# Dilated-attention projections regrouped from twelve 384-wide blocks to nine 512-wide ones, with both query tiles of a head pair scored together

## The chip, the cores and the metric

The kernel runs on one core of a Trainium2 chip. The metric is the device time in microseconds (us) of one launch; the compute engines of the core are TensorE (PE, its weight loads are listed as PEld), VectorE (DVE), ScalarE (ACT) and GpSimd (POOL), and SyncE (SP) issues the DMA transfers. A lower time is better.

## What is computed

Four transformer-like layers work on one activation `x` of 256 rows by 1024 columns in float32: one attention layer, one retention layer (each with a gated feed-forward part), and then two "hybrid" layers. Only the hybrid layers are touched here. One hybrid layer, cut to what matters:

```
h = rmsnorm(x, norm_g)
proj = h @ w_in                                  # 1024 x 11168
a_b, a_c, a_x, a_z, c_q, c_kv, k_pe, b_z, dq, dk, dv, c_z, gate_pre = split(proj)
# a: gated short convolution, b: latent attention (MLA)
# c: dilated attention: 3 groups (dilation 1, 4, 16) x 8 heads x 64
dq = rmsnorm(dq per head); dk = rmsnorm(dk per head)
for g in 3 groups:                               # causal, ALiBi bias, window/dilation
    o_g, lse_g = dilated_group_attention(dq[g], dk[g], dv[g], slopes[g], dilation_g)
o_c = sum_g softmax_g(lse_g) * o_g               # = one softmax over the keys of all groups
y_c = o_c * silu(c_z)
merged = g_a*(y_a @ w_out_a) + g_b*(y_b @ w_out_b) + g_c*(y_c @ w_out_c)
x = x + merged @ w_o
```

The columns `dq`, `dk` and `dv` are 1536 each: 3 groups by 8 heads by 64. The change concerns how these 4608 columns are projected and how the dilated heads are scored.

## The kernel before

The 256 rows are two row tiles `t` of 128. Every large product is computed in three passes of split float32 (a high and a low part of both operands; `mm3` issues high by high, high by low, low by high). The activation `h` is the operand that is loaded (128x128) and the weights stream past it, 512 or 384 or 416 columns at a time, into one PSUM bank of 512 float32 columns; there are eight banks (`bank`, tag `p`). A weight block is loaded by SP in raw chunks (`raw`, line 325, two buffers), and ACT makes the high part (`whi`, line 345) and DVE the low part (`wlo`, line 346) in pieces of up to 1024 elements a partition; eight pieces are held at once (`WB`).

`gemm_col` walks over the blocks of columns: for each block, row tile 0 and then row tile 1, eight k steps of three matmuls each. When a row tile of a block is complete, its epilogue (`epi`) is spawned as a job, a Python generator, which issues some work and then yields a planned delay (`D_DQ`, `D_SOFTD`, ...). The PE's order is that in which the program issues its instructions: a planner adds the modelled time of every matmul to a clock, and after each `mm3` the jobs whose time is due issue their next piece, so that small matmuls and transposes (`trs`, line 281, one 128x128 transpose for each 128 columns) are interleaved between the large ones. PE executes exactly this order and waits where an operand is not ready; the other engines' order is made by a scheduler from the same program order.

In a hybrid layer `first_half` does the convolution and the MLA branch. Then `dilated` runs over four head pairs `pr`. For each pair there are three weight blocks of 384 columns (3 groups by 128): q, k and v. The q and k epilogues square the bank (ACT, `dsq`), sum by head (DVE, `dss`), take the inverse root (POOL, line 452), scale into `rows` (DVE), and `D_DQ` = 7.82 planned us later transpose `rows` (3 transposes) into `dq` or `dk`, with even and odd sequence positions apart. The v epilogue copies the bank (`dvn`) and two DMAs separate even and odd rows into `dv`. `dq`, `dk`, `dv` have two buffers each.

When all epilogues of a pair are done, `dil_pair` spawns `dil_heads` for query tile 0 (even positions), and 2 * `SP_DIL` = 9 planned us later for tile 1 (odd positions). One `dil_heads` scores both heads of the pair: 8 matmuls of 64 rows by 128 columns, which the profile shows as 16 (float32 runs as two), into two banks; the heads sit on partitions 0 to 63 and 64 to 127, so two run side by side. Then for each head there is bias and maximum (DVE, line 1388), exponential with sum (ACT, line 1390), reciprocal, scaling (ACT, line 1392) into `dsm`, and `D_SOFTD` = 5.7 planned us after the scores four transposes for head 0 and, `D_SOFTD2` = 2.2 later, four for head 1, copied to `daT`. The values product of a tile (again 16 matmuls in the profile, 64 columns of output each, `p<-daT,dv`) is issued when that tile's job is done. `ocT` receives the pair's result; it is needed in the third branch, after the blocks `c_z` of the projection.

After the dilated blocks come 512-wide blocks of the same projection: `b_z` (epilogue due after `D_Z` = 12.44), two gate blocks, and so on.

Of the kernel before, what the change touches and what calls it, by code (L numbers as in the profile page):

```python
# [21 lines left out]
NEG = -1e30  # L22
BIG = 1e30
WB = 8
AT0, DSM, DAT, GT = 8, 4, 4, 2
# [7 lines left out]
D_EV0, D_ROT0, D_SOFT, D_SB = 5.11, 5.49, 11.39, 9.42  # L33
D_ADA0, D_ADAF, D_ADA1, D_FFN, D_FFN1 = 12.84, 50.82, 20.9, 11.5, 11.36
D_ROT, D_GG, D_B0, D_Q, D_K, D_EV, D_SOFTM = 9.55, 13.08, 3.75, 17.27, 6.36, 5.2, 8.78
D_DQ, D_SOFTD, D_SOFTD2, D_Z, D_MERGE = 7.82, 5.7, 2.2, 12.44, 1.98
SP_SB, SP_MB, SP_MLA, SP_DIL = 2.55, 2.65, 13.59, 4.5

def _r(a, b):
    return list(range(a, b))
# [14 lines left out]
B_CONV, B_GA, B_DIL, B_ZB, B_GB, B_ZC, B_GC = 1, 5, 7, 19, 20, 22, 23  # L57
# [177 lines left out]
DIL_COLS = [[(0, 1), (0, 0), (1, 0), (2, 0)], [(0, 1), (1, 1), (2, 1), (0, 0)]]  # L235
# [9 lines left out]
class Kern:  # L245
# [1068 lines left out]

    def dilated(self, q, gqk, ocT):
        V, A, wk = self.V, self.A, self.wk
        pj = []
        for pr in range(4):
            dq, dk = (q.tile([128, 3, 256], F32, tag=n, bufs=2, name=self.nm(n)) for n in ("dq", "dk"))
            dv = q.tile([128, 2, 384], F32, tag="dv", bufs=2, name=self.nm("dv"))  # L1320
            b0 = B_DIL + 3 * pr
            eo = lambda x, t: x.rearrange("p g (r t i) -> p g t r i", r=2, t=2)[:, :, t]

            def epi(b, t, _, ps, b0=b0, dq=dq, dk=dk, dv=dv):
                if b - b0 == 2:
# [4 lines left out]
                    return  # L1330
                sq = wk.tile([128, 512], F32, tag="rtmp", name=self.nm("dsq"))
                ss = wk.tile([128, 8], F32, tag="dss", bufs=4, name=self.nm("dss"))
                rows = wk.tile([128, 512], F32, tag="rows", bufs=4, name=self.nm("rows"))
                A.activation(sq[:, :384], ps, AF.Square, scale=0.125)  # L1334
                V.tensor_reduce(ss[:, :6], sq[:, :384].rearrange("p (h d) -> p h d", d=64), AX.X, ALU.add)  # L1335
                self.rstd(ss[:, :6], 6, 1e-6)
                V.tensor_tensor(rows[:, :384].rearrange("p (h d) -> p h d", d=64), ps.rearrange("p (h d) -> p h d", d=64),  # L1337
                                ss[:, :6, None].to_broadcast([128, 6, 64]), ALU.mult)
                yield D_DQ
                src = self.trs(rows, 3).rearrange("p g (i r) -> p g r i", r=2)  # L1340
                if b == b0:
                    A.copy(eo(dq, t), src)
                else:
                    V.tensor_tensor(eo(dk, t), src, gqk[:, :, None, None].to_broadcast([128, 3, 2, 64]), ALU.mult)

            jb = self.gemm_col(self.h, self.key, self.chs[b0:b0 + 3], epi, b0)
            pj.append(self.spawn(self.dil_pair(pr, dq, dk, dv, ocT, jb), 0.5))
        return pj

    def dil_pair(self, pr, dq, dk, dv, ocT, deps):  # L1350


        tabs = []
# [19 lines left out]
        self.A.copy(ocT[:, pr].rearrange("p (n r) -> p r n", r=2), pv[:, :256].rearrange("p (r n) -> p r n", r=2))  # L1373

    def dil_heads(self, t, dq, dk, tabs, aTs):


        V, A = self.V, self.A
        ps = [self.bank() for _ in range(2)]
        for i, (g, k) in enumerate(DIL_COLS[t]):  # L1380
            for j, o in enumerate((0, 64)):
                self.mm(ps[j][:, i * 128:i * 128 + 128], dq[o:o + 64, g, t * 128:t * 128 + 128],
                        dk[o:o + 64, g, k * 128:k * 128 + 128], us=0.12)
        sms = []
        for j in range(2):
            st = self.wk.tile([128, 6], F32, tag="st", bufs=8, name=self.nm("dst"))
            sm = self.ph.tile([128, 512], F32, tag="dsm", bufs=DSM, name=self.nm("dsm"))
            V.tensor_tensor_reduce(sm, ps[j], tabs[j][:, t * 128:t * 128 + 512], 1.0, NEG, ALU.add, ALU.max, st[:, 0:1])  # L1388
            V.tensor_scalar_mul(st[:, 2:3], st[:, 0:1], -0.125)  # L1389
            A.activation(sm, sm, AF.Exp, bias=st[:, 2:3], scale=0.125, accum_out=st[:, 3:4])  # L1390
            V.reciprocal(st[:, 3:4], st[:, 3:4])
            A.activation(sm, sm, AF.Copy, scale=st[:, 3:4])  # L1392
            sms.append(sm)
        yield D_SOFTD
        for j in range(2):
            aT = self.ph.tile([128, 4, 128], F32, tag="daT", bufs=DAT, name=self.nm("daT"))
            A.copy(aT, self.trs(sms[j], 4))
            aTs[t, 64 * j] = aT
            yield D_SOFTD2 if j == 0 else 1.5


def build(tc, a, stop=99):
# [67 lines left out]
```

## Time and profile before

| | before |
|---|---|
| runs, us | 1496.15, 1497.75, 1500.12 |
| median, us | 1497.75 |
| profiled execution: time, us | 1494.65 |
| profiled execution: span of the instructions, us | 1492.9 |
| busy share of PE, DVE, ACT, POOL | 98%, 69%, 53%, 6% |
| PE instructions | 7508 |
| mean granted TensorE clock | 0.993 |

The span is the time from the first to the last instruction in the profiled execution; that execution's own time has a little added around it. A matmul's row in the timeline has its start and its length, and successive matmuls overlap, so the time that one takes from the stream is the distance from its start to the next start, not its length. In the names, `p<-whi,hh` means that the bank `p` is written from the weights `whi` and the activation `hh`.

### The profile page before, as it was taken

To read this page: it belongs to the slowest core of one execution; us is meant where nothing else is said; L and a number is where in the kernel's file an instruction comes from. 1 tells how busy PE (TensorE), PEld (TensorE's weight loads), DVE (VectorE), ACT (ScalarE), POOL (GpSimd) and SP (SyncE) were. 2 spreads that over 40 slices of the span, in tenths; PEclk is the share of its full clock that TensorE was granted. 3 is DMA by queue.
4 is the path that set the end of the run, shared out by engine and by line. 5 is a ranking of instruction groups with operands and counts; after the bars stand their busy time and mean duration, and the time that the engine had idled before them with its cause. 6 is when DMAs were issued, how large, how long until landed. Compare 5 with 4: busy or idle time off the path is not lost.

```text
span 1492.9 us, 19658 instructions
## 1 busy us (share of the span) xinstructions
PE 1458.3 (98%) x7508; PEld 1213.2 (81%) x7508; DVE 1022.9 (69%) x1605; ACT 793.8 (53%) x1297; POOL 96.3 (6%) x84
## 2 busy tenths in 40 slices
PE   7999999999999999999999999999999999999998
PEld 4776788887877888888887889988888889998887
DVE  4688887846988849755378655566676865656664
ACT  4657555533444535554266745566445674566551
POOL 0000000000000000000012011110001201111000
PEclk9999999999999999999999999999999999999999
DMA  9757587755776638645445455554635535555552
GB/s 379 273 177 275 193 324 285 285 199 184 279 276 231 258 137 279 256 174 197 155 144 180 146 170 178 181 202 154 220 135 200 190 121 194 171 179 198 184 174 80
DMA packets 52961, 306.62 MB, mean 205 GB/s; under 512 B 7546, under 2 KB 10490, under 8 KB 24580
## 3 DMA queue, kind: packets, MB, share of 16 engines
q1 hardware_dynamic: 52148, 305.14, 57.2%
q8 instruction: 59, 0.97, 0.3%
q10 hardware_dynamic: 720, 0.24, 0.1%
q14 instruction: 34, 0.28, 0.1%
HBM read 301.16 MB, written 1.05 MB: 202 GB/s over the span
## 4 chain that ended last, share of the span: by engine, by line
PE 75%; DVE 11%; ACT 5%; DMA 4%; POOL 3%; issue 2%; POOLq 0%; SPq 0%; DVEq 0%; ACTq 0%
PE p L277 71%; DVE wlo L346 5%; PE p L281 4%; DMA raw<-in_w_in_dram 3%; POOL dss L452 2%; ACT dsm L1390 1%; ACT whi L345 1%; DVE dsm L1388 1%; ACT dsm L1392 1%; DVE dss L1335 1%; POOL qss L452 1%; DVE junk L493 0%; DVE rows L1337 0%; ACT dsq L1334 0%; DVE res L520 0%
## 5 line engine op out<-in xcount | busy, mean ns | idle before, releaser
L346 DVE TENSOR_TENSOR wlo<-raw,whi 128x1024 fp32r<-128x1024 f32 (+2 forms) x474 | 539.6, 1161 | 163.5 <-ACT whi L345 158.1
L345 ACT CAST whi<-raw 128x1024 fp32r<-128x1024 f32 (+2 forms) x474 | 464.4, 1002 | 276.3 <-PE p L277 191.4
L277 PE MATMUL p<-whi,hh 128*128 128x512 f32 (+1 forms) x1504 | 590.9, 393 | 5.0 <-ACT mqT L1223 2.0
L277 PE MATMUL p<-whi,hl 128*128 128x512 f32 (+1 forms) x1504 | 568.3, 378 | 3.2 <-DVE hl L457 2.7
L277 PE MATMUL p<-wlo,hh 128*128 128x512 f32 (+1 forms) x1504 | 566.7, 377 | 0.0
L277 PEld LDWEIGHTS p<-whi,hh 128*128 128x128 f32 x1504 | 284.1, 189 | 55.3 <-issue 8.7
L277 PEld LDWEIGHTS p<-whi,hl 128*128 128x128 f32 x1504 | 283.8, 189 | 50.0 <-DVE hl L457 3.9
L277 PEld LDWEIGHTS p<-wlo,hh 128*128 128x128 f32 x1504 | 284.6, 189 | 40.9 <-issue 1.7
L541 DVE SCALAR_TENSOR_TENSOR acc<-raw,csc,acc 128x1024 f32<-128x1024 f32 x80 | 102.3, 1278 | 4.6 <-DMA raw<-in_ada_w_dram 4.3
L277 PE MATMUL p<-whi,ah 128*128 128x512 f32 x176 | 70.0, 398 | 0.0
L277 PE MATMUL p<-whi,al 128*128 128x512 f32 x176 | 69.5, 395 | 0.0
L277 PE MATMUL p<-wlo,ah 128*128 128x512 f32 x176 | 69.5, 395 | 0.0
L452 POOL TENSOR_TENSOR dss<-dss,mh 128x6 f32<-128x6 f32 x32 | 46.2, 1443 | 331.1 <-DVE dss L451 331.1
L916 ACT ACTIVATE fth<-p 128x256 f32<-128x256 f32 x44 | 16.9, 383 | 69.3 <-PE p L277 69.3
L1337 DVE TENSOR_TENSOR rows<-p,dss 128x384 f32<-128x384 f32 x32 | 17.8, 557 | 46.3 <-POOL dss L452 46.3
L1390 ACT ACTIVATE dsm<-dsm,dst 128x512 f32<-128x512 f32 x32 | 22.9, 716 | 40.8 <-DVE dst L1389 40.8
L485 POOL TENSOR_TENSOR ss<-ss,mh 128x1 f32<-128x1 f32 x14 | 13.5, 962 | 479.3 <-DVE ss L484 479.3
L277 PE MATMUL p<-whi,s 128*128 128x512 f32 x128 | 41.3, 397 | 0.0
L277 PEld LDWEIGHTS p<-whi,al 128*128 128x128 f32 x176 | 33.0, 187 | 8.1
L277 PEld LDWEIGHTS p<-wlo,ah 128*128 128x128 f32 x176 | 33.0, 188 | 7.8
L277 PEld LDWEIGHTS p<-whi,ah 128*128 128x128 f32 x176 | 33.0, 188 | 7.8
L277 PE MATMUL p<-whi,yh 128*128 128x512 f32 x96 | 38.4, 400 | 0.0
(251 smaller groups left out, 1522.3 us busy)
## 6 DMA issues: line engine op xcount, KB each, us to landing
raw<-in_w_in_dram SPq DMA_DIRECT2D x48, 1024.0 KB, 4.9
raw<-in_w_gu_dram SPq DMA_DIRECT2D x44, 1024.0 KB, 5.1
raw<-in_ada_w_dram SPq DMA_DIRECT2D x40, 1024.0 KB, 6.3
raw<-in_w_in_dram SPq DMA_DIRECT2D x48, 768.0 KB, 4.4
raw<-in_w_ret_dram SPq DMA_DIRECT2D x24, 1024.0 KB, 5.0
raw<-in_w_dn_dram SPq DMA_DIRECT2D x22, 1024.0 KB, 4.9
raw<-in_w_qkv_dram SPq DMA_DIRECT2D x11, 1024.0 KB, 5.5
as<-in_ada_s_dram SPq DMA_DIRECT2D x16, 512.0 KB, 8.0
```

The costliest lines, as they stand in the source:

```text
L277: self.T.matmul(out, lhsT=lhsT, rhs=rhs, start=first, stop=last, skip_group_check=skip)
L281: self.T.transpose(out, in_, self.ident)
L345: for ins in (self.A.copy(hi[:, :m * n], src), self.V.tensor_tensor(lo[:, :m * n], src, hi[:, :m * n].bitcast(F32), ALU.subtract)):
L346: self.V.tensor_tensor(lo[:, :m * n], src, hi[:, :m * n].bitcast(F32), ALU.subtract)):
L452: self.G.tensor_tensor(ss, ss, self.mh[:, :n], ALU.pow)
L541: self.V.scalar_tensor_tensor(acc, r[:, j * D:j * D + D], self.sc[:, k:k + 1], acc, ALU.mult, ALU.add)
L916: A.activation(th, ps[:, 0:256], AF.Silu)
L1335: V.tensor_reduce(ss[:, :6], sq[:, :384].rearrange("p (h d) -> p h d", d=64), AX.X, ALU.add)
L1337: V.tensor_tensor(rows[:, :384].rearrange("p (h d) -> p h d", d=64), ps.rearrange("p (h d) -> p h d", d=64), ss[:, :6, None].to_broadcast( ...
L1388: V.tensor_tensor_reduce(sm, ps[j], tabs[j][:, t * 128:t * 128 + 512], 1.0, NEG, ALU.add, ALU.max, st[:, 0:1])
L1390: A.activation(sm, sm, AF.Exp, bias=st[:, 2:3], scale=0.125, accum_out=st[:, 3:4])
L1392: A.activation(sm, sm, AF.Copy, scale=st[:, 3:4])
```

## The change

The nine (p, s, g) units of a head pair (q, k, v by three groups, 128 columns each) are put one after the other for all four pairs, 36 units in all, and cut into nine blocks of four units, 512 columns, in place of twelve blocks of 384. One epilogue serves a block with any mix of q, k and v units of one or two pairs: the q and k units of a block (4, 2, 3, 3, 2, 4, 1, 4 and 1 of them) are squared, normalised and transposed together, and then copied run by run into the buffers of their pair; v units are copied and sent by DMA run by run. A pair starts when all epilogues of the blocks that hold one of its units are done, that is after blocks 2, 4, 6 and 8.

`dil_heads` is gone. A pair issues the scores of both query tiles in one stretch (four banks, 32 matmuls as the profile counts them), the softmax of its four heads one behind the other, then the four groups of four transposes, the first `D_SOFTD` = 6.8 planned us after the scores and the others 2.4 apart, and then the values of both tiles in one stretch (32 matmuls). No arithmetic is changed.

```diff
-D_DQ, D_SOFTD, D_SOFTD2, D_Z, D_MERGE = 7.82, 5.7, 2.2, 12.44, 1.98
-SP_SB, SP_MB, SP_MLA, SP_DIL = 2.55, 2.65, 13.59, 4.5
+D_DQ, D_SOFTD, D_SOFTD2, D_Z, D_MERGE = 7.82, 6.8, 2.4, 12.44, 1.98
+SP_SB, SP_MB, SP_MLA = 2.55, 2.65, 13.59
...
-for _p in range(4):
-    for _b in (2976, 4512, 6048):
-        IN_BLOCKS.append([_b + g * 512 + _p * 128 + j for g in range(3) for j in range(128)])
+DIL_UNITS = [(p, s, g) for p in range(4) for s in range(3) for g in range(3)]
+for _i in range(0, 36, 4):
+    IN_BLOCKS.append([(2976, 4512, 6048)[s] + g * 512 + p * 128 + j for p, s, g in DIL_UNITS[_i:_i + 4]
+                      for j in range(128)])
...
+        def buf(p, s):
+            if (p, s) not in bufs:
+                bufs[p, s] = q.tile([128, 2, 384] if s == 2 else [128, 3, 256], F32, tag=("dq", "dk", "dv")[s], bufs=2,
+                                    name=self.nm("dqkv"))
+            return bufs[p, s]
+
+        def epi(b, t, _, ps):
+            units = DIL_UNITS[4 * (b - B_DIL):4 * (b - B_DIL) + 4]
...
+            A.activation(sq[:, :nu * 128], src, AF.Square, scale=0.125)
+            V.tensor_reduce(ss[:, :2 * nu], d3(sq[:, :nu * 128]), AX.X, ALU.add)
+            self.rstd(ss[:, :2 * nu], 2 * nu, 1e-6)
+            for i, (p, s), g, n in runs:
+                if s == 2:
                     nat = q.tile([128, 384], F32, tag="dvn", bufs=2, name=self.nm("dvn"))
-                    A.copy(nat, ps)
+                    A.copy(nat[:, :n * 128], ps[:, cs(i, n)])
                     for r in range(2):
-                        self.nc.sync.dma_start(dv[64 * t:64 * t + 64, r], nat[r:128:2])
...
+                        self.nc.sync.dma_start(buf(p, 2)[64 * t:64 * t + 64, r, cs(g, n)], nat[r:128:2, :n * 128])
+            V.tensor_tensor(d3(rows[:, :nu * 128]), d3(src), ss[:, :2 * nu, None].to_broadcast([128, 2 * nu, 64]), ALU.mult)
+            yield D_DQ
+            tp = self.trs(rows, nu).rearrange("p g (i r) -> p g r i", r=2)
...
+        for b in range(9):
+            jb = self.gemm_col(self.h, self.key, self.chs[B_DIL + b:B_DIL + b + 1], epi, B_DIL + b)
...
+            for p in range(4):
+                if 4 * b < 9 * p + 9 <= 4 * b + 4:
+                    pj.append(self.spawn(self.dil_pair(p, buf(p, 0), buf(p, 1), buf(p, 2), ocT, jobs[p]), 0.5))
         return pj
...
-        aTs, jobs = {}, []
+        ps, sms, aTs = {}, {}, {}
         for t in range(2):
-            jobs.append(self.spawn(self.dil_heads(t, dq, dk, tabs, aTs)))
-            yield 2 * SP_DIL if t == 0 else 0.5
+            for o in (0, 64):
+                ps[t, o] = self.bank()
+            for i, (g, k) in enumerate(DIL_COLS[t]):
+                for o in (0, 64):
+                    self.mm(ps[t, o][:, i * 128:i * 128 + 128], dq[o:o + 64, g, t * 128:t * 128 + 128],
+                            dk[o:o + 64, g, k * 128:k * 128 + 128], us=0.12)
+        for t in range(2):
+            for o in (0, 64):
+                st = self.wk.tile([128, 6], F32, tag="st", bufs=8, name=self.nm("dst"))
+                sm = self.ph.tile([128, 512], F32, tag="dsm", bufs=DSM, name=self.nm("dsm"))
+                V.tensor_tensor_reduce(sm, ps[t, o], tabs[o // 64][:, t * 128:t * 128 + 512], 1.0, NEG, ALU.add, ALU.max,
+                                       st[:, 0:1])
+                V.tensor_scalar_mul(st[:, 2:3], st[:, 0:1], -0.125)
+                A.activation(sm, sm, AF.Exp, bias=st[:, 2:3], scale=0.125, accum_out=st[:, 3:4])
+                V.reciprocal(st[:, 3:4], st[:, 3:4])
+                A.activation(sm, sm, AF.Copy, scale=st[:, 3:4])
+                sms[t, o] = sm
+        yield D_SOFTD
+        for t in range(2):
+            for o in (0, 64):
+                aTs[t, o] = self.ph.tile([128, 4, 128], F32, tag="daT", bufs=DAT, name=self.nm("daT"))
+                A.copy(aTs[t, o], self.trs(sms[t, o], 4))
+                yield D_SOFTD2
         pv = self.bank()
         for t in range(2):
-            while not jobs[t].done:
-                yield 0.5
             for i, (g, k) in enumerate(DIL_COLS[t]):
```

## Rows read from the trace of the kernel before

**Rows 1.** The page: busy time of PE and of the other engines.
```profile
PE 1458.3 (98%) x7508; PEld 1213.2 (81%) x7508; DVE 1022.9 (69%) x1605; ACT 793.8 (53%) x1297; POOL 96.3 (6%) x84
```

**Rows 2.** Stretch of the first dilated stage: length, busy PE, PEld, DVE, ACT, POOL, clock.
```profile
874.70:1010.00 135.30, 134.18 (x910) 126.65 (x909) 81.92 (x163) 77.74 (x137) 23.10 (x16) 1.00 0.57 192
```

**Rows 3.** PE's waits, first stage (one row), second stage: total, times, longest, us.
```profile
PE p L281 <- DVE rows L1337: 1.1, 1, 1.1
...
PE p L281 <- DVE rows L1337: 0.8, 1, 0.8
PE p L277 <- DVE dk L1344: 0.3, 1, 0.3
```

**Rows 4.** PE timeline: two stretches, 384 wide (66 matmuls) and 512 wide (48).
```profile
875.76 0.33 PE L277 MATMUL p<-whi,hh 128*128 128x384 f32 x1
...
887.02 0.33 PE L277 MATMUL p<-whi,hl 128*128 128x384 f32 x1
...
786.31 0.40 PE L277 MATMUL p<-whi,hh 128*128 128x512 f32 x1
...
796.99 0.39 PE L277 MATMUL p<-whi,hl 128*128 128x512 f32 x1
```

**Rows 5.** PE timeline: two more 512-wide stretches, 182 and 36 matmuls.
```profile
1031.27 0.40 PE L277 MATMUL p<-wlo,hh 128*128 128x512 f32 x1
...
1072.70 0.39 PE L277 MATMUL p<-whi,hl 128*128 128x512 f32 x1
...
862.17 0.40 PE L277 MATMUL p<-whi,yh 128*128 128x512 f32 x1
...
870.34 0.39 PE L277 MATMUL p<-whi,yl 128*128 128x512 f32 x1
```

**Rows 6.** PE timeline: around a score group; its last 12 and 4 matmuls.
```profile
903.47 0.34 PE L277 MATMUL p<-whi,hl 128*128 128x384 f32 x1
...
905.12 0.34 PE L277 MATMUL p<-wlo,hh 128*128 128x384 f32 x1
...
904.06 0.84 PE L277 MATMUL p<-dk,dq 64*128 64x128 f32 x12
...
904.51 0.39 PE L277 MATMUL p<-dk,dq 64*128 64x128 f32 x4
```

**Rows 7.** PE timeline: around a values group; its last 14 and 8 matmuls.
```profile
917.65 0.34 PE L277 MATMUL p<-whi,hl 128*128 128x384 f32 x1
...
919.22 0.33 PE L277 MATMUL p<-wlo,hh 128*128 128x384 f32 x1
...
918.08 0.93 PE L277 MATMUL p<-daT,dv 128*64 128x128 f32 x14
...
918.41 0.61 PE L277 MATMUL p<-daT,dv 128*64 128x128 f32 x8
```

**Rows 8.** SP's longest wait in the first stage: us in total, times, longest.
```profile
SPq L325 <- DVE wlo L346: 87.2, 22, 8.7
```

**Rows 9.** The last pair's result in the first hybrid layer, and its first reader.
```profile
1030.66 0.40 ACT L1373 COPY ocT<-p 128x256 f32<-128x256 f32 x1 [0.68 <-PE p L277]
...
1079.42 1.22 DVE L1069 TENSOR_TENSOR ocT<-ocT,zT 128x1024 f32<-128x1024 f32 x1 [0.39 <-ACT zT L1062]
```

**Rows 10.** ACT timeline: start of a softmax of two heads, and the epilogue behind it.
```profile
973.22 0.72 ACT L1390 ACTIVATE dsm<-dsm,dst 128x512 f32<-128x512 f32 x1 [2.07 <-DVE dst L1389]
...
975.88 0.47 ACT L1334 ACTIVATE dsq<-p 128x384 f32<-128x384 f32 x1
```

**Rows 11.** PE timeline: the late epilogue of the first dilated stage.
```profile
998.66 0.34 PE L277 MATMUL p<-whi,hl 128*128 128x384 f32 x1
1000.12 0.55 PE L281 MATMUL p<-ident,rows 128*128 128x128 f32 x3 [1.12 <-DVE rows L1337]
```

**Rows 12.** DVE timeline: the weight pieces that stood ahead of that epilogue.
```profile
992.38 4.62 DVE L346 TENSOR_TENSOR wlo<-raw,whi 128x1024 fp32r<-128x1024 f32 x4
```

**Rows 13.** Group of the first softmax step on DVE, first stage: busy us, mean ns.
```profile
L1388 DVE CUSTOM_DVE_ANT_0 dsm<-p,dtab 128x512 f32<-128x512 f32 x12 | 7.8, 685 | 0.5 <-PE p L277 0.5
```

More of the change, by code (lines that the diff above doesn't have):

```diff
@@ L51 @@
 IN_BLOCKS += [_r(8096, 8608), _r(8608, 9120)]
-for _p in range(4):
-    for _b in (2976, 4512, 6048):
-        IN_BLOCKS.append([_b + g * 512 + _p * 128 + j for g in range(3) for j in range(128)])
+DIL_UNITS = [(p, s, g) for p in range(4) for s in range(3) for g in range(3)]
+for _i in range(0, 36, 4):
+    IN_BLOCKS.append([(2976, 4512, 6048)[s] + g * 512 + p * 128 + j for p, s, g in DIL_UNITS[_i:_i + 4]
+                      for j in range(128)])
 IN_BLOCKS += [_r(2464, 2976), _r(9120, 9632), _r(9632, 10144)]
 IN_BLOCKS += [_r(7584, 8096), _r(10144, 10656), _r(10656, 11168)]
-B_CONV, B_GA, B_DIL, B_ZB, B_GB, B_ZC, B_GC = 1, 5, 7, 19, 20, 22, 23
+B_CONV, B_GA, B_DIL, B_ZB, B_GB, B_ZC, B_GC = 1, 5, 7, 16, 17, 19, 20
 UQ_BLOCKS = [_r(0, 768)]
@@ L1316, in dilated @@
         V, A, wk = self.V, self.A, self.wk
[L1317 to L1325, printed above, removed]
+        pj, jobs, bufs = [], {}, {}
@@ new lines, in dilated @@
+        eo = lambda x, g, n, t: x.rearrange("p g (r t i) -> p g t r i", r=2, t=2)[:, g:g + n, t]
+        def buf(p, s):
[5 more added lines that the diff above has]
+            units = DIL_UNITS[4 * (b - B_DIL):4 * (b - B_DIL) + 4]
+            runs = []
+            for i, (p, s, g) in enumerate(units):
+                if runs and runs[-1][1] == (p, s):
+                    runs[-1][3] += 1
+                else:
+                    runs.append([i, (p, s), g, 1])
+            cs = lambda i, n: slice(i * 128, (i + n) * 128)
+            qk = [i for i, u in enumerate(units) if u[1] < 2]
+            u0, nu = qk[0], len(qk)
+            sq = wk.tile([128, 512], F32, tag="rtmp", name=self.nm("dsq"))
+            ss = wk.tile([128, 8], F32, tag="dss", bufs=4, name=self.nm("dss"))
+            rows = wk.tile([128, 512], F32, tag="rows", bufs=4, name=self.nm("rows"))
+            src = ps[:, cs(u0, nu)]
+            d3 = lambda x: x.rearrange("p (h d) -> p h d", d=64)
+            A.activation(sq[:, :nu * 128], src, AF.Square, scale=0.125)
[3 more added lines that the diff above has]
+                if s == 2:
@@ L1326, in epi @@
                     nat = q.tile([128, 384], F32, tag="dvn", bufs=2, name=self.nm("dvn"))
-                    A.copy(nat, ps)
+                    A.copy(nat[:, :n * 128], ps[:, cs(i, n)])
                     for r in range(2):
-                        self.nc.sync.dma_start(dv[64 * t:64 * t + 64, r], nat[r:128:2])
-                    return
-                sq = wk.tile([128, 512], F32, tag="rtmp", name=self.nm("dsq"))
-                ss = wk.tile([128, 8], F32, tag="dss", bufs=4, name=self.nm("dss"))
@@ L1333, in epi @@
[L1333 to L1342, printed above, removed]
-                else:
-                    V.tensor_tensor(eo(dk, t), src, gqk[:, :, None, None].to_broadcast([128, 3, 2, 64]), ALU.mult)
-            jb = self.gemm_col(self.h, self.key, self.chs[b0:b0 + 3], epi, b0)
-            pj.append(self.spawn(self.dil_pair(pr, dq, dk, dv, ocT, jb), 0.5))
+                        self.nc.sync.dma_start(buf(p, 2)[64 * t:64 * t + 64, r, cs(g, n)], nat[r:128:2, :n * 128])
@@ new lines, in epi @@
+            V.tensor_tensor(d3(rows[:, :nu * 128]), d3(src), ss[:, :2 * nu, None].to_broadcast([128, 2 * nu, 64]), ALU.mult)
+            yield D_DQ
+            tp = self.trs(rows, nu).rearrange("p g (i r) -> p g r i", r=2)
+            for i, (p, s), g, n in runs:
+                if s == 2:
+                    continue
+                part = tp[:, i - u0:i - u0 + n]
+                if s == 0:
+                    A.copy(eo(buf(p, 0), g, n, t), part)
+                else:
+                    V.tensor_tensor(eo(buf(p, 1), g, n, t), part,
+                                    gqk[:, g:g + n, None, None].to_broadcast([128, n, 2, 64]), ALU.mult)
@@ L1348, in dilated @@
+        for b in range(9):
+            jb = self.gemm_col(self.h, self.key, self.chs[B_DIL + b:B_DIL + b + 1], epi, B_DIL + b)
+            for p, _, _ in DIL_UNITS[4 * b:4 * b + 4]:
+                jobs.setdefault(p, []).extend(j for j in jb if j not in jobs.get(p, []))
+            for p in range(4):
+                if 4 * b < 9 * p + 9 <= 4 * b + 4:
+                    pj.append(self.spawn(self.dil_pair(p, buf(p, 0), buf(p, 1), buf(p, 2), ocT, jobs[p]), 0.5))
         return pj
     def dil_pair(self, pr, dq, dk, dv, ocT, deps):
+        V, A = self.V, self.A
@@ L1372, in dil_pair @@
                             aTs[t, o][:, i], t == 0 and i == 0, i == 3, 0.109, True)
[L1373 to L1399, printed above, removed]
+        A.copy(ocT[:, pr].rearrange("p (n r) -> p r n", r=2), pv[:, :256].rearrange("p (r n) -> p r n", r=2))
 def build(tc, a, stop=99):
```

## The prediction, made before the change was run

> **What bounds the kernel now.** I read the page first, to see which engine is full: PE is busy for 98% of the span, DVE for 69%, ACT for 53% [rows 1]. A full engine by average says little of one stage, so the next view is the busy time by stretch. The two dilated stages are of about 135 us each and alike; in the first, PE is busy for 134.2 of 135.3 us at the full granted clock, while DVE and ACT have 53 and 58 us free [rows 2]. Then the waits of PE there: 1.1 us in the first stage and 0.8 and 0.3 in the second, 2.2 in all [rows 3]. So in these stages the end is set by what PE has to issue, and nearly every microsecond that its stream loses or gains comes back in the time. Since matmuls overlap, a cost on PE is read as a distance between starts, never as a length, and the price of a small group is the distance between the large matmul before it and the second large one after it, less two ordinary steps. All costs below are read that way.
>
> **The projection, the largest part.** The change replaces 12 blocks of 384 columns by 9 of 512 in each of two layers. A block is 8 k steps, 3 passes and 2 row tiles, 48 matmuls: 1152 matmuls of 384 columns become 864 of 512, with the same number of columns, 442,368. In 65 steps of the 384-wide stream pass 11.26 us, 0.1732 each; 1152 of them are 199.6 us [rows 4]. For 512 wide with the same loaded operand `h` there are two stretches, 0.2272 (47 steps in 10.68 us) and 0.2289 (181 steps in 41.43) [rows 4, 5]. I take the middle, 0.228: 864 steps are 197.0 us, so the projection saves 2.6 us. The ends are 196.3 (a gain of 3.3) and, if the new blocks step like the stretch with another loaded operand, 0.2334 (35 steps in 8.17), 201.7 us, a loss of 2.1 [rows 5]. The point for the reader: a matmul that is a third wider costs a third more to within 1.3%. Fewer matmuls are not less work here.
>
> At this place a rule can be weighed. The rows say that four 384-wide matmuls (0.693 us) give way to three 512-wide ones (0.684), 9 ns less. The Trainium skill, "TensorE: Matmul & The Clock Gate", section "Wait — 56ns, not 53.3ns?", has a warm matmul cost one cycle per column and about 2.5 ns besides; by it each such exchange would save 2.5 ns, an estimate of 0.7 us over the 288 matmuls that go. The trace's steps are longer than that rule's for both widths, and the sum goes by the rows.
>
> **Scores.** Each of the eight pairs scored its query tiles in two groups of 16; now it is one of 32. A group of 16 costs 905.12 - 903.47 - 2 x 0.173 = 1.30 us of the stream, while inside it eight matmuls, from the last 12 to the last 4, take 0.45 [rows 6], so 16 more in an open group cost 0.90. What is spared is 0.40 us of entering and leaving, eight times: 3.2 us. The ends are nothing, if both halves pay the entry all the same, or if the second group shares its entry with transposes already, and 3.2.
>
> **Values.** These too go from two groups of 16 to one of 32 per pair. A group costs 919.22 - 917.65 - 0.35 = 1.22, and six matmuls inside it 0.33, so 16 cost 0.88 [rows 7]. That is 0.34 spared, eight times: 2.7 us; the ends are 0 and 2.7.
>
> **What I cost at nothing.** The transposes: 24 units of q and k in each row tile before and after, in 18 epilogues a layer in place of 16, and 16 groups of four for the softmax as before. The weights: as many elements in 36 pieces a layer instead of 48; SP waited 87 us of the stage for a free raw buffer behind DVE [rows 8], so loads run ahead of their use, and no wait for a weight piece is among the PE waits [rows 3]. A block now holds the stream for 11 us where it held it for 8.3, which gives the loads more time. Were that cover gone, PE would show waits for `wlo`, at most a load's cast and subtraction each time. The two more epilogues, four more runs of `dvn` with their eight more DMAs on SP's queue ahead of weight loads, and the split copies into `dq` and `dk` lie in DVE's and ACT's free 53 and 58 us [rows 2] and in SP's slack. The last pair starts later, because its block now has transposes to wait for; its result was ready 49 us before its reader [rows 9].
>
> **What moves.** The scores of a pair come when the epilogues of its last block have been transposed, some 9 planned us after that block's end. Behind them the softmax of four heads, not two, sits on DVE and ACT in one piece. Two heads held ACT for 975.88 - 973.22 = 2.66 us before the next epilogue's square began [rows 10]; four hold it for about 5.3. Behind it in ACT's order wait the squares of the block that ends meanwhile, and behind those `rows` and its transposes, for which PE waits in program order. By my estimate row tile 1 of the next block ends about 4 us after the scores begin (10.9 us of matmuls and about 2.2 of scores, against 9 planned) and so falls in that stretch for pairs 0, 1 and 2; the last pair is followed by the `b_z` block, whose epilogue has the longer `D_Z`. The first group of softmax transposes is due 6.8 planned us after the scores, in place of 5.7. The bounds for these waits are none and, at six places, the 2.7 us by which the softmax grew with the 1.29 by which one epilogue was late already (1000.12 - 998.66 - 0.17, behind four weight pieces of 4.62 us) [rows 11, 12]: 4.0 each, 24 us. I take the lower region, the 2.2 us of before again: the planned 7.82 us were enough for all but two epilogues of 32 [rows 3], and there is now one softmax per pair where there were two that could get in the way.
>
> **The sum.** 2.6 + 3.2 + 2.7 = 8.5 us less. The profiled execution took 1494.65 us, 1.75 around its span of 1492.9; it would take 1486.1. It lies 3.1 below the median of the three runs, 1497.75, and from that median the forecast is 1489.2.
>
> **Rivals.**
> *The wide steps are the slow ones.* If the new blocks step at 0.2334, the projection loses 2.1 instead of saving 2.6, and 3.8 us are left: 1493.9. For it speaks that such a step stands in the trace [rows 5]; against it, that there the loaded operand was another tile.
> *The softmax of four heads makes epilogues late.* This one ends slower. At six places PE waits for `rows`, 4.0 us each as above: 1489.2 - 2.2 + 24.0 = 1511.0. The gain is gone from 10.7 / 6 = 1.8 us a place, and it is a loss of more than 4.5 us from 2.5 a place. For it speak the doubled softmax with only 1.1 planned us more before its transposes, and that weight pieces are all of the 1024 kind now, whose four held DVE for 4.6 us [rows 12]; against it, that these waits were few.
> *The score banks come free too late.* A pair now fills four of the eight banks at once, and DVE empties them at 0.685 each [rows 13]: the last of four is free 1.4 us later than the last of two. If PE has to wait for it, eight pairs lose 11 us: 1500.2. The Trainium skill, "TensorEngine Tiling (Array Packing)", section "PSUM Bottleneck", says that matmuls running side by side do not speed up the emptying of PSUM. No wait of PE in the trace is for a bank [rows 3].
> *Nothing comes of it*, because another engine sets the end of the stage: with so few waits of PE [rows 3] it is hardly possible on the way down.
>
> **How the numbers follow.** 0.3% of this time, 4.5 us, is about what a measurement of this kernel can tell from no change. The forecast has a chance of 0.62; the slow steps 0.13 and the late banks 0.05, both within 0.3%; late epilogues 0.20, of which 0.13 beyond the loss of 4.5 us and 0.07 before it. That gives 0.62 for faster, 0.25 for the same and 0.13 for slower. The lower end of the range takes the projection's 3.3, all of both merges, and no waits left (2.2): 11.4 us, 1486.3; I round it to 1485 for the runs' own spread of 4 us. The upper end leaves out no more than the slower part of the late epilogues: 1500, where the late banks end too. For the forecast alone it is 1485 to 1493.
>
> **What would show it.** In the profile after, 864 steps of 0.227 to 0.229 between starts, where 0.233 is the first rival; eight score groups of 32 at about 2.2 us of the stream and eight values groups at about 2.1; PE waits for `rows` or `dsm` in these two stages that sum to about 2 us, where over 10 is the second rival; no wait of PE that a line-1388 instruction ends, or the third is at work. The prediction would be wrong if those waits grow, or if the layers outside the dilated stages change by more than a microsecond.

## The result, and the profile after

| | before | after |
|---|---|---|
| median of six runs, us | 1497.26 | 1509.35 |
| lowest and highest, us | 1492.16, 1500.12 | 1503.14, 1512.09 |
| profiled execution: time, us | 1494.65 | 1510.99 |
| mean granted TensorE clock in it | 0.993 | 0.985 |

The ratio of after to before is 1.008, with an interval of 1.0065 to 1.0095: the change makes the kernel slower, by 12.1 us between the medians. The forecast was 1489.2 with a range to 1500; the time that came is within 2 us of the second rival's 1511.0.

The first part of the profile's page after the change. PE has 288 matmuls less, and DVE and ACT are as busy as in [rows 1]:

```profile
PE 1461.6 (97%) x7220; PEld 1181.1 (78%) x7220; DVE 1021.1 (68%) x1601; ACT 793.7 (53%) x1293; POOL 93.7 (6%) x88
```

**Where the time went.** A dilated stage with its neighbours is measured from the last matmul of the convolution's product to the first of the next branch's; both are named `p<-whi,yl`. PE's timeline of the kernel before:

```profile
874.46 0.39 PE L277 MATMUL p<-whi,yl 128*128 128x512 f32 x1
...
1043.12 0.39 PE L277 MATMUL p<-whi,yl 128*128 128x512 f32 x1
...
1240.49 0.39 PE L277 MATMUL p<-whi,yl 128*128 128x512 f32 x1
...
1409.28 0.39 PE L277 MATMUL p<-whi,yl 128*128 128x512 f32 x1
```

and of the kernel after:

```profile
877.61 0.39 PE L279 MATMUL p<-whi,yl 128*128 128x512 f32 x1
...
1053.54 0.39 PE L279 MATMUL p<-whi,yl 128*128 128x512 f32 x1
...
1251.01 0.39 PE L279 MATMUL p<-whi,yl 128*128 128x512 f32 x1
...
1425.50 0.39 PE L279 MATMUL p<-whi,yl 128*128 128x512 f32 x1
```

The stages took 168.66 and 168.79 us and take 175.93 and 174.49: 7.27 and 5.70 longer, 13.0 together. Between them pass 197.4 us before and 197.5 after. The first stage begins 3.15 us later in this execution, since PE's clock was at half for 13.7 us in the first matmuls of the kernel, in place of 6.8 before; that is ahead of anything the change touches, and the medians differ by less than the two profiled executions do (12.1 against 16.3).

PE's waits, the view of [rows 3], first stage and second stage after:

```profile
PE p L283 <- DVE rows L1354: 4.4, 2, 2.4
PE p L283 <- DVE dss L453: 3.3, 1, 3.3
...
PE p L283 <- DVE rows L1354: 4.4, 2, 2.4
PE p L283 <- DVE dss L453: 3.4, 1, 3.4
```

Each stage has three waits, all ahead of the transposes of `rows`; 15.5 us in all where 2.2 stood. For the third the list names `dss` of line 453, DVE's next instruction, which ended just behind `rows`. In PE's timeline the first and the third of them are:

```profile
933.95 0.39 PE L279 MATMUL p<-whi,hl 128*128 128x512 f32 x1
936.77 0.87 PE L283 MATMUL p<-ident,rows 128*128 128x128 f32 x3 [2.43 <-DVE rows L1354]
...
1000.75 0.39 PE L279 MATMUL p<-whi,hl 128*128 128x512 f32 x1
1004.48 0.71 PE L283 MATMUL p<-ident,rows 128*128 128x128 f32 x4 [3.35 <-DVE dss L453]
...
1005.41 0.63 PE L279 MATMUL p<-wlo,hh 128*128 128x512 f32 x1
...
1007.12 0.63 PE L279 MATMUL p<-whi,hl 128*128 128x512 f32 x1
```

By starts, less one step of 0.23, the stream loses 2.59 and 3.50 us there; the six places lose 2.59, 2.17, 3.50 and 2.58, 2.18, 3.51, together 16.5. The last two rows show a second loss. From 1005.41 to 1007.12 are four steps, 0.43 each, where the same matmuls take 0.228 elsewhere. The windows of the kernel after say why (start and end, length, busy PE, PEld, DVE, ACT, POOL, granted clock, DMA share, GB/s):

```profile
936.60:940.00 3.40, 3.23 (x9) 2.58 (x10) 2.13 (x4) 1.04 (x1) 0.40 (x1) 0.50 0.82 308
940.10:960.00 19.90, 19.90 (x144) 16.40 (x143) 11.36 (x25) 9.93 (x18) 2.64 (x2) 1.00 0.43 150
1004.90:1008.30 3.40, 3.40 (x13) 2.74 (x11) 2.47 (x4) 1.42 (x2) 0.35 (x1) 0.50 0.30 104
1307.00:1311.00 4.00, 1.57 (x10) 1.05 (x9) 2.21 (x8) 1.33 (x2) 2.30 (x2) 1.00 0.39 90
1311.00:1339.00 28.00, 28.00 (x182) 22.94 (x181) 16.61 (x33) 17.88 (x33) 2.64 (x2) 1.00 0.49 173
```

After the wait the clock is at its lower level, 1.2 GHz, for 3.4 us. This follows five of the six waits (also at 970.8, 1342.8 and 1376.9) and not the one at 1307. A stretch of 3.4 us at half clock does 1.7 us of work, so the five cost about 8.5 us; by the steps (0.43 for 0.228) it is 8.0. In the six runs the mean clock and the time go together: 0.991 with 1503.14 us, 0.985 with 1510.99 and 1512.09.

The sum closes to 0.2 us: 16.5 of waits and 8.5 of clock, less 11.85, are 13.15 for the 13.0 of the stages. The 11.85 are what the two stages gain when nothing waits, as the version with a later due time below shows. By the runs below they are 9.3 us of PE's own work (6.2 from the merged groups and 3.1 from the projection, where 8.5 was priced), and 2.6 us of waits that the kernel before had in these stages (1.29 and 0.98 at `rows`, 0.3 at `dk`).

**What was late.** ACT ahead of the third wait, the kernel after: the softmax of four heads, three weight casts, then the square of the block that had ended meanwhile:

```profile
990.97 0.72 ACT L1404 ACTIVATE dsm<-dsm,dst 128x512 f32<-128x512 f32 x1 [3.94 <-DVE dst L1403]
...
995.04 1.32 ACT L1406 ACTIVATE dsm<-dsm,dst 128x512 f32<-128x512 f32 x2
996.27 2.94 ACT L347 CAST whi<-raw 128x1024 fp32r<-128x1024 f32 x3
999.11 0.58 ACT L1345 ACTIVATE dsq<-p 128x512 f32<-128x512 f32 x1
```

then DVE, and POOL between DVE's sum and its scaling:

```profile
997.33 3.50 DVE L348 TENSOR_TENSOR wlo<-raw,whi 128x1024 fp32r<-128x1024 f32 x3 [2.00 <-ACT whi L347]
1000.74 0.68 DVE L1346 TENSOR_REDUCE dss<-dsq 128x8 f32<-128x512 f32 x1
...
1003.64 0.69 DVE L1354 TENSOR_TENSOR rows<-p,dss 128x512 f32<-128x512 f32 x1 [1.63 <-POOL dss L454]
```

```profile
1001.98 1.64 POOL L454 TENSOR_TENSOR dss<-dss,mh 128x8 f32<-128x8 f32 x1 [14.18 <-DVE dss L453]
```

The softmax holds ACT from 990.97 to 996.27, the 5.3 us that the prediction had estimated. Behind it stand things that the prediction did not add up: 2.94 us of casts ahead of the square, the subtractions (3.50) that end at 1000.7 ahead of the sum, and 1.64 on POOL.

**What the prediction wanted to see.** The 512-wide step, in a stretch of the new blocks (30 steps), PE's timeline after:

```profile
1024.09 0.40 PE L279 MATMUL p<-whi,hl 128*128 128x512 f32 x1
...
1030.91 0.39 PE L279 MATMUL p<-whi,hl 128*128 128x512 f32 x1
```

That is 0.2273 us a step, and 0.2288 in 17 steps from 893.29 on. A score group of 32 and a values group of 32, each with the large matmul before it and the second one behind it:

```profile
922.75 0.40 PE L279 MATMUL p<-whi,hl 128*128 128x512 f32 x1
923.08 2.06 PE L279 MATMUL p<-dqkv,dqkv 64*128 64x128 f32 x32
...
925.40 0.40 PE L279 MATMUL p<-wlo,hh 128*128 128x512 f32 x1
...
980.59 0.39 PE L279 MATMUL p<-whi,hl 128*128 128x512 f32 x1
980.90 1.97 PE L279 MATMUL p<-daT,dqkv 128*64 128x128 f32 x32
...
983.14 0.40 PE L279 MATMUL p<-wlo,hh 128*128 128x512 f32 x1
```

Read as in [rows 6, 7] with two steps of 0.228 taken off, they cost 2.19 and 2.09 us; 2.2 and 2.1 were forecast.

### The profile page after: what moved, and what is told of

Its sections match the earlier page's. It is cut to its first block, busy times and chain, and to the rows that moved or that the text cites. A ratio compares the mean times of both kernels' runs of the same rounds, so it can differ in the third digit from the quotient of the medians.

```text
span 1509.2 us, 19098 instructions
## 1 busy us (share of the span) xinstructions
PE 1461.6 (97%) x7220; PEld 1181.1 (78%) x7220; DVE 1021.1 (68%) x1601; ACT 793.7 (53%) x1293; POOL 93.7 (6%) x88
## 4 chain that ended last, share of the span: by engine, by line
PE 82%; DVE 7%; ACT 5%; issue 2%; POOL 2%; DMA 2%; SPq 0%; DVEq 0%; POOLq 0%; ACTq 0%
PE p L279 77%; PE p L283 4%; DVE wlo L348 3%; ACT whi L347 2%; ACT dsm L1404 1%; DMA raw<-in_w_in_dram 1%; POOL dss L454 1%; ACT dsm L1406 1%; DVE dsm L1401 0%; DVE dss L1346 0%; POOL qss L454 0%; DVE junk L495 0%; DMA raw<-in_w_ao_dram 0%; DVE res L522 0%; DVE acc L543 0%
## 5 line engine op out<-in xcount | busy, mean ns | idle before, releaser
L348 DVE TENSOR_TENSOR wlo<-raw,whi 128x1024 fp32r<-128x1024 f32 x450 | 538.9, 1215 | 184.4 <-ACT whi L347 178.7
L347 ACT CAST whi<-raw 128x1024 fp32r<-128x1024 f32 x450 | 463.6, 1045 | 292.2 <-PE p L279 220.0
L279 PEld LDWEIGHTS p<-whi,hh 128*128 128x128 f32 x1408 | 268.1, 190 | 63.6 <-issue 7.7
L279 PEld LDWEIGHTS p<-whi,hl 128*128 128x128 f32 x1408 | 268.0, 190 | 63.1 <-DVE hl L459 3.9
L279 PEld LDWEIGHTS p<-wlo,hh 128*128 128x128 f32 x1408 | 268.5, 191 | 50.1 <-issue 1.7
L454 POOL TENSOR_TENSOR dss<-dss,mh 128x8 f32<-128x8 f32 (+3 forms) x36 | 43.7, 1217 | 354.8 <-DVE dss L453 354.8
L1354 DVE TENSOR_TENSOR rows<-p,dss 128x512 f32<-128x512 f32 (+3 forms) x36 | 18.4, 513 | 43.7 <-POOL dss L454 41.3
L283 PE MATMUL p<-ident,rows 128*128 128x128 f32 x160 | 26.6, 281 | 19.2 <-DVE rows L1354 8.9
L283 PEld LDWEIGHTS p<-ident,rows 128*128 128x128 f32 x160 | 19.9, 143 | 26.8 <-issue 22.5
L1346 DVE TENSOR_REDUCE dss<-dsq 128x8 f32<-128x512 f32 (+3 forms) x36 | 17.8, 503 | 32.1 <-ACT dsq L1345 32.1
```

The costliest lines, as they stand in the source:

```text
L279: self.T.matmul(out, lhsT=lhsT, rhs=rhs, start=first, stop=last, skip_group_check=skip)
L283: self.T.transpose(out, in_, self.ident)
L347: for ins in (self.A.copy(hi[:, :m * n], src), self.V.tensor_tensor(lo[:, :m * n], src, hi[:, :m * n].bitcast(F32), ALU.subtract)):
L348: self.V.tensor_tensor(lo[:, :m * n], src, hi[:, :m * n].bitcast(F32), ALU.subtract)):
L454: self.G.tensor_tensor(ss, ss, self.mh[:, :n], ALU.pow)
L1346: V.tensor_reduce(ss[:, :2 * nu], d3(sq[:, :nu * 128]), AX.X, ALU.add)
```

## The experiments

The theory is this. The softmax of four heads, which sits on ACT and DVE in one piece with weight pieces behind it, makes the epilogue of row tile 1 of the block that follows (blocks 3, 5 and 7) late against an unchanged `D_DQ`; the waits, and the half clock behind them, are the loss, and PE's own work is cheaper as priced. The rivals: the wide steps or the merged groups cost more than they spare; a later due time would have helped the kernel before as well; the clock has nothing to do with the waits.

The kernel before had a median of 1495.99 us beside four of the versions (the later due time, two softmaxes, only the wide blocks, only the joint pair), 1497.22 beside the next four (three epilogues, useless work, a shorter softmax, the epilogue first) and 1496.81 beside the last two. The ratios, with their 95% intervals in brackets, are the recorded ones to runs of the kernel before; they differ by up to 0.0011 from the quotients of these medians. Stage lengths are read as above. The edits are against the changed kernel, the last one against the kernel before; left-out lines are marked by dots.

**A later due time.** All dilated epilogues are given 12 planned us.

```diff
-D_DQ, D_SOFTD, D_SOFTD2, D_Z, D_MERGE = 7.82, 6.8, 2.4, 12.44, 1.98
+D_DQ, D_SOFTD, D_SOFTD2, D_Z, D_MERGE = 12.0, 6.8, 2.4, 12.44, 1.98
```

> The changed kernel with the epilogues' transposes due 12.0 planned us after the block instead of 7.82 (D_DQ), nothing else. Theory (late rows): the changed kernel loses its time at three places a layer where PE waits 2.2 to 3.5 us for rows that stand behind the softmax of four heads, and in a stretch of 3.4 us at half clock after five of these six waits; due 4 us later, the rows are ready, no wait over 0.5 us and no half clock is left in the two dilated stages, and the time is 1497.3 - 8.5 - 3.8 = 1485 us. Rival (the wider blocks and the merged groups are themselves slower than priced): the waits go but the time stays over 1495 us.

It took 1483.13 us, ratio 0.9907 [0.9892, 0.9922]. The window of its first stage (columns as above):

```profile
877.00:1040.00 163.00, 163.00 (x957) 134.24 (x956) 99.84 (x187) 99.42 (x167) 21.94 (x18) 1.00 0.52 184
```

PE is busy throughout, at the full clock. Both stages take 162.80 us, 5.86 and 5.99 less than before. All of the loss hangs on the waits, and what the change is worth without them is 11.85 us, the waits of before included. This version has the lowest median of all, ahead of both kernels; against the next version its lead of 0.8 us is within the noise.

**The same for three epilogues only**, those that the theory names.

```diff
-            yield D_DQ
+            yield D_DQ + (4.0 if t == 1 and b - B_DIL in (3, 5, 7) else 0.0)
```

> The changed kernel with the transposes of three epilogues a layer alone (row tile 1 of the dilated blocks 3, 5 and 7) due 4.0 planned us later; all else, the moment of the scores too, stays as it was. Theory (all that is lost is the PE waiting at these six places, and the half clock after them): no wait over 0.5 us, no half clock in the two stages, 1483 to 1487 us, as with every epilogue due later. Rival (a later due time helped because it moved the scores, too, to another moment of the block): waits and half clock stay, over 1500 us.

1483.89 us, ratio 0.9922 [0.9893, 0.9951]; no wait and no half clock in the stages, 162.74 us each. Three epilogues of 18 in a layer carry the whole loss.

**Two softmaxes again.** The second query tile's softmax is issued 4.5 planned us after the first one's; the joint scores stay.

```diff
+D_HALF = 4.5
...
         for t in range(2):
+            if t:
+                yield D_HALF
             for o in (0, 64):
...
-        yield D_SOFTD
+        yield D_SOFTD - D_HALF
```

> The changed kernel with the scores of a pair still in one stretch, but the softmax of the second query tile issued 4.5 planned us after that of the first; transposes due as before. Theory (late rows, because four heads sit in one piece ahead of the squares): the squares of the block that ends meanwhile go ahead of the second half, the six waits shrink from 2.2 to 3.5 us to under 1 us each, few or no half-clock stretches, 1485 to 1491 us. Rival (the phase: a block of 512 that starts its pair after its own transposes always ends its next row tile at the wrong moment, however the softmax is cut): waits of 2 us and more stay, 1503 to 1510 us.

1486.61 us, ratio 0.993 [0.9915, 0.9945]. One wait of 0.6 us is left in each stage and no stretch at half clock; the stages take 163.55 and 163.59. That the softmax stands in one piece matters, as the theory says.

**A shorter softmax.** The reciprocal and the scaling on ACT go.

```diff
-                V.reciprocal(st[:, 3:4], st[:, 3:4])
-                A.activation(sm, sm, AF.Copy, scale=st[:, 3:4])
```

> The changed kernel without the last step of the dilated softmax, the reciprocal and the scaling by it (its values stay unnormalised): four ACT instructions of 0.7 us each and their round trips through DVE are gone from the piece that stands ahead of the squares. Theory (rows are late by what the softmax in one piece and the weight pieces behind it hold up on ACT and DVE): the waits shrink by about 2.6 us each, two of three places a layer go to nothing and the third to about 1 us, no half clock, 1484 to 1490 us. Rival (the rows are late for what stands on DVE and POOL alone): the waits stay over 1.5 us, over 1500 us.

1485.44 us, ratio 0.9919 [0.9897, 0.9942]; 0.7 us of waits in each stage, no half clock, stages of 163.83 and 163.80. This too is on the theory's side.

**Only the wide blocks**, with the scores, softmax and values of the kernel before.

```diff
-D_DQ, D_SOFTD, D_SOFTD2, D_Z, D_MERGE = 7.82, 6.8, 2.4, 12.44, 1.98
-SP_SB, SP_MB, SP_MLA = 2.55, 2.65, 13.59
+D_DQ, D_SOFTD, D_SOFTD2, D_Z, D_MERGE = 7.82, 5.7, 2.2, 12.44, 1.98
+SP_SB, SP_MB, SP_MLA, SP_DIL = 2.55, 2.65, 13.59, 4.5
...
+            jobs.append(self.spawn(self.dil_heads(t, dq, dk, tabs, aTs)))
+            yield 2 * SP_DIL if t == 0 else 0.5
...
```

> One part of the change alone: nine blocks of 512 with their mixed epilogues, but each query tile scored, softmaxed and multiplied by its own job as in the kernel before (two score groups and two values groups a pair). Theory (late rows behind four heads): with two heads in a piece no wait over 1 us; the projection's 2.6 us are gained, 1493 to 1496 us. Rival (phase or width): waits of 2 us and more at the same six places with half clock after them, 1505 us or more.

1490.84 us, ratio 0.9962 [0.9947, 0.9977], 2 us faster than the theory's range; there is no wait, and both stages take 165.89. Against the later due time's 162.80 the merged scores and values are worth 3.09 us a layer; they were priced at 2.95. Against before, the blocks gain 2.77 and 2.90, of which the waits of before are 1.3 each; the projection itself gives some 3.1 us in two layers, priced at 2.6. The first rival is out.

**Only the joint pair**, with the twelve 384-wide blocks.

```diff
-DIL_UNITS = [(p, s, g) for p in range(4) for s in range(3) for g in range(3)]
-for _i in range(0, 36, 4):
...
+for _p in range(4):
+    for _b in (2976, 4512, 6048):
+        IN_BLOCKS.append([_b + g * 512 + _p * 128 + j for g in range(3) for j in range(128)])
...
```

> The other part alone: twelve blocks of 384 as before, but both query tiles of a pair scored in one group, four heads softmaxed in one piece, values in one group. Theory (late rows behind four heads): waits for rows of 1 to 3 us behind most of the eight softmaxes, more than the 5.9 us that the merges spare: 1499 to 1512 us. Rival (phase or width of the new blocks): no such waits, the merges' 5.9 us are gained, 1490 to 1493 us.

1493.38 us, ratio 0.998 [0.9968, 0.9992]. This is a miss: the theory wanted a loss, and the time came out on the rival's side, 0.4 us above its range. PE's waits in the first stage:

```profile
PE p L281 <- DVE rows L1337: 2.7, 3, 0.9
PE p L277 <- DVE dk L1344: 1.4, 1, 1.4
```

The three places are there, with about 1 us each, and no half clock follows them. ACT of that kernel around the first place:

```profile
914.90 0.47 ACT L1334 ACTIVATE dsq<-p 128x384 f32<-128x384 f32 x1
915.28 3.02 ACT L345 CAST whi<-raw 128x768 fp32r<-128x768 f32 x4
918.20 0.48 ACT L1334 ACTIVATE dsq<-p 128x384 f32<-128x384 f32 x1
```

So the softmax of four heads alone, 5.3 us here too (909.61 to 914.90), does not make the loss. With 384 columns the blocks end at other moments of it: one square follows the softmax at once, the late one behind four casts. The pieces of 768 elements are shorter as well. Which of the two matters more was not tried. PE's rows show the moments: the first of these epilogues has its `rows` ready at 918.86 and PE comes to them at 919.50; PE comes to the late one about 14 us after the softmax began, where the three late ones of the changed kernel's first stage were wanted 8 to 10 us after it. The theory as first put is too short: the loss takes both parts of the change together. The stage's own sum fits, with the merges' gain of 2.95 and 3.0 us more waits (4.1 for 1.1): 168.79 us against 168.66 (in the second stage 2.7 us of waits, and 167.40 against 168.79).

**Useless work in the waits.** 22, 16 and 28 matmuls of 128 columns, into a spare bank, stand ahead of the three late groups of transposes.

```diff
             yield D_DQ
+            fill = {3: 22, 5: 16, 7: 28}.get(b - B_DIL, 0) if t == 1 else 0
+            if fill:
+                spare = self.bank()
+                for i in range(fill):
+                    self.mm(spare[:, 0:128], self.h(0, 0)[0], self.h(1, 0)[0], us=0.0)
```

> The changed kernel with 22, 16 and 28 useless matmuls of 128 columns (2.4, 1.7 and 3.0 us of PE work whose result nobody reads) put ahead of the three late transposes of each layer, so that PE works through most of a wait it has anyway. Theory (part of the loss is the half clock that follows an idle PE): the rows come as late as before, but no half clock follows, and the time falls by 1.7 us for each of the five to six stretches, to 1498 to 1502 us. Rival (the waits alone are the loss and the clock rows mean nothing for the time): 1507 to 1512 us.

1500.52 us, ratio 1.002 [1.0007, 1.0033]. PE's timeline at the first place, and the window of the stage:

```profile
930.18 0.39 PE L279 MATMUL p<-whi,hl 128*128 128x512 f32 x1
930.40 2.57 PE L279 MATMUL p<-hh 128*128 128x128 f32 x22
932.99 0.52 PE L283 MATMUL p<-ident,rows 128*128 128x128 f32 x3
...
874.00:1045.00 171.00, 170.43 (x1022) 141.32 (x1021) 99.40 (x187) 99.24 (x167) 21.85 (x18) 1.00 0.51 175
```

At the first place the transposes start as late as before (2.81 us behind the last large matmul here, 2.82 without the useless work), PE works instead of waiting, and the clock stays at 1.00. The stages take 171.34 and 171.30 us, 4.59 and 3.19 less than after: 7.8 in all for the five stretches, 1.6 each. With work that does nothing the kernel is faster (ratio 1.002 to before where it was 1.008), so the second loss is the clock's, and it follows from the idle PE. The Trainium skill, "TensorE: Matmul & The Clock Gate", section "Terms", takes the penalty of a throttled time as that time multiplied by one minus the ratio of the clocks; for five stretches of 3.4 us that makes an estimate of 8.5 us, with which the measured 7.8 agrees to within a tenth.

**The epilogue first.** The epilogue up to `rows` is put ahead of other work on its engines.

```diff
+            with self.first():
-            A.activation(sq[:, :nu * 128], src, AF.Square, scale=0.125)
+                A.activation(sq[:, :nu * 128], src, AF.Square, scale=0.125)
...
```

> The changed kernel with the instructions of each dilated epilogue up to its rows put ahead of other ready work in the order of ACT, DVE and POOL (the same raised priority that the norms have); due times as in the changed kernel. Theory (rows wait in order behind work that could wait: the softmax in one piece and the casts of weight pieces): the squares and sums go ahead, the six waits fall under 1 us each, no half clock, 1483 to 1489 us. Rival (rows are late because the chain square, sum, POOL, scale is itself too long for 7.82 planned us): the waits stay at 2 to 3.5 us, 1505 us or more.

1487.03 us, ratio 0.9933 [0.9913, 0.9954]. No wait for `rows` is left; one of 1.0 us (0.9 in the second stage) for `daT` takes their place, in the first stage:

```profile
PE p L279 <- ACT daT L1413: 1.0, 1, 1.0
```

The stages take 164.46 and 164.45. The chain is quick enough by itself; what stands ahead of it makes it late.

**The softmax first too.** As above, and the softmax of the four heads has the same precedence: only the weight pieces go behind both.

```diff
+        with self.first():
-        for t in range(2):
+            for t in range(2):
...
```

> The changed kernel with both the dilated epilogues and the softmax of the four heads raised above other ready work, so that between these two the order is that of the program again and only other work, the casts of weight pieces above all, goes behind. Theory (the softmax in one piece and the weight pieces that pile up behind it each make up about half of the lateness): the softmax still stands ahead of the squares, but the pieces do not; the waits shrink from 2.2 to 3.5 us to 1.5 us or less each, no half clock, 1484 to 1491 us. Rival (the softmax alone holds the rows up): the waits stay at 2 us and more, over 1500 us.

1491.27 us, ratio 0.9964 [0.9946, 0.9981], 0.3 us above the theory's range. Its waits in the second stage:

```profile
PE p L283 <- DVE rows L1355: 1.6, 2, 1.4
PE p L279 <- ACT daT L1414: 0.8, 1, 0.8
```

With the softmax still ahead of the epilogue but the weight pieces behind it, 1.6 us of waits for `rows` remain of 7.8, and no half clock follows. The lateness needs both the long softmax and the weight pieces. Either one taken away leaves 0.6 to 1.7 us of the 7.8 a stage: 0.6 with two softmaxes, 0.7 with the shorter one, 1.6 and 1.7 here. How it divides between them, which the theory put at about half each, is not shown.

**The later due time in the kernel before.**

```diff
-D_DQ, D_SOFTD, D_SOFTD2, D_Z, D_MERGE = 7.82, 5.7, 2.2, 12.44, 1.98
+D_DQ, D_SOFTD, D_SOFTD2, D_Z, D_MERGE = 12.0, 5.7, 2.2, 12.44, 1.98
```

> The kernel before with its q and k transposes due 12.0 planned us after the block instead of 7.82, nothing else: a control for the due time. Theory (the kernel before loses about 1.9 us a stage to late rows, and the rest of what the later due time gave the changed kernel is the change's own 8.5 us): 3 to 4 us less than before, 1493 to 1495 us. Rival (a later due time is worth more than the waits that it ends): 1488 us or less.

1499.21 us, ratio 1.0018 [1.0001, 1.0035]. This is a miss as well: a small gain was expected. The expectation was also misread from the rows: it has 1.9 us of late rows a stage, where 1.9 is the sum of both stages [rows 3]. PE's waits in the first stage:

```profile
PE p L281 <- ACT dsm L1392: 2.5, 3, 1.0
PE p L277 <- DVE dk L1344: 0.4, 1, 0.4
```

The waits for `rows` are gone, and more came at the softmax's transposes, whose due times were left as they were (2.9 us of waits in the first stage and 3.1 in the second, for 1.1 and 1.1); the stages take 170.86 us, 2.1 to 2.2 longer. The 12.0 planned us are no gain by themselves; they pay with the change. Other due times in the kernel before were not tried, but PE's waits in its two stages are 2.2 us on the list and 2.6 by starts, with no half clock behind them, so ending them could not have brought the 12.9.

## Why the prediction was wrong

- *The stage is bound by what PE issues.* Right: with the waits taken away PE is busy for 163.00 of 163.00 us, and the gain comes out.
- *The projection, 2.6 us.* Right in kind and a little low: it is some 3.1 by the run of the wide blocks alone, and the step is 0.2273 to 0.2288, in the forecast 0.228. One reading was wrong: the stretch of 182 matmuls in [rows 5], taken for one with `h` alone, has 48 with another loaded operand in it (`yh`, `yl`, from 1042.65 to 1053.85). Its steps with `h` take 0.2273, by which the projection would have been priced at a gain of 3.2.
- *Scores and values, 3.2 and 2.7.* Right: 6.2 for 5.9, and 2.19 and 2.09 us a group.
- *What was costed at nothing.* No wait of PE in the two stages is for a weight piece or a DMA, and the stretch between the stages is as long as before. But the weight pieces were weighed only as operands of PE. They also stand in ACT's and DVE's order ahead of the epilogue, and there they cost: 2.94 us of casts and 3.50 of subtractions at the third place.
- *The waits.* This is the step that failed: "I take the lower region, the 2.2 us of before again: the planned 7.82 us were enough for all but two epilogues of 32". That epilogues were in time says nothing of their margin, and the change doubled the softmax that stands ahead of three of them per layer. The trace of the kernel before had the margins. In its first stage five of the 16 epilogues, all behind a softmax, had their `rows` ready at most 0.5 us before PE began to transpose them. One of them, with 0.05 us to spare (DVE's row, then PE's):

```profile
991.91 0.56 DVE L1337 TENSOR_TENSOR rows<-p,dss 128x384 f32<-128x384 f32 x1 [1.50 <-POOL dss L452]
992.52 0.55 PE L281 MATMUL p<-ident,rows 128*128 128x128 f32 x3
```

The sum that was not made, with the rows of after at the first place: the large matmul at 922.75 is the last before the scores, the softmax holds ACT from 926.11 to 931.41, and the chain behind it (a cast of 1.03, the square, a subtraction of 1.23, the sums, 2.29 on POOL, the scaling) lets the transposes start at 936.77, 14.0 us after that matmul. PE had come to them at 934.2, 11.4 after it. That there is one softmax per pair in place of two was taken for a relief; the one that is left is longer, and the epilogues behind it are late.
- *The clock.* It is no term of the prediction at all. About 8.5 us, a third of the loss at the six places, is the half clock after the waits.
- *The second rival* named the place, the number of places and the sum: 4.0 us at six against (16.5 + 8.5) / 6 = 4.2. Its parts were others. It had 2.7 for the softmax's growth and 1.29 for lateness that was there already; measured are 2.75 of wait and 1.4 of clock, and the joint softmax without the wide blocks made only about 1 us a place. That the sum agrees so well is in part luck. Its chance of 0.20 was too low for what spoke for it: a burst twice as long, larger weight pieces, the same due time.
- *The third rival*: no wait of PE is for a bank.

So the gain did not vanish. PE's work became cheaper by about what was forecast (9.3 us for 8.5), and the waits and the clock behind them took more than that. Open is why the joint softmax makes the epilogues less late with 384-wide blocks: the order of ACT's rows and the later moments at which PE wants the `rows` are read from the trace, and neither was tested by itself.

## What to carry to other kernels

When small jobs are merged, add up the in-order queues between the last input and the next planned use (the longer burst, what the scheduler puts behind it, the chain itself) and hold that against the due time; a list of waits tells which operands were late, never how near the others were; for that, compare the end of each operand with the start of its use. Retune the due times with the merge: here 12.0 in place of 7.82 turns 12.1 us of loss into 12.9 of gain, while in the kernel before the same number gains nothing. And price a wait of a busy PE above its own length, as the clock may fall behind it.

## What the runs showed of the hardware

Five of six idle stretches of PE of 2.2 to 3.5 us were followed by 3.4 us at a granted clock of 0.50, in which a 512-wide step takes 0.43 us and not 0.228. After the wait of 2.58 us at 1307 the clock stayed at 1.00. In the dilated stages none followed the waits of at most 1.4 us in the kernel before, the joint pair alone or the two versions with precedence, and none where PE was given useless work in the same place.

The length of a wait does not decide it by itself. Between the two stages every version has one such wait of 2.5 to 2.9 us, for `junk`; in seven of the twelve profiled executions, that of the kernel before among them, 3.4 us at half clock followed it, and in five not. The kernel before after 2.55 us, and the version with useless work after 2.88 us (columns as above):

```profile
1131.00:1134.40 3.40, 3.40 (x11) 2.79 (x10) 2.38 (x7) 1.63 (x9) 0.70 (x1) 0.51 0.64 192
...
1132.20:1136.00 3.80, 3.80 (x21) 3.25 (x22) 2.92 (x7) 2.12 (x9) 0.70 (x1) 1.00 0.69 202
```
